# A two-layer transformer trunk step: 62 modulation units go from VectorE to TensorE, and their weight loads are placed anew

## The chip, the cores and the metric

One core of one Trainium2 chip runs the whole program. The metric is the device time of one execution in microseconds (us). The engines are named as in the profile: PE is TensorE (matmuls; PEld its weight loads), DVE is VectorE, ACT is ScalarE, POOL is GpSimd, and SP is SyncE, whose queue issues nearly all transfers.

## The reference, cut to what matters

The trunk has two layers. Each layer is a feed-forward half, a token mixer, and a second feed-forward half. 640 tokens (512 latent, 128 context) have 1024 features. Ahead of every sub-layer its input is modulated, and its output is gated:

```python
def _modulation(cond, w, b):
    return (jax.nn.silu(cond) @ w + b).reshape(cond.shape[0], N_MOD, D_MODEL)

def _modulate(x, shift, scale):
    return x * (1.0 + scale[:, None, :]) + shift[:, None, :]

def _residual_post_norm(x, f, gate, weight, g, b):
    return _layernorm(DN_ALPHA * x + weight * gate[:, None, :] * f, g, b)

def _ffn_half(x, mod, slot, w1, w3, w2, g, b):
    h = _modulate(x, mod[:, 3 * slot], mod[:, 3 * slot + 1])
    f = (jax.nn.silu(h @ w1) * (h @ w3)) @ w2
    return _residual_post_norm(x, f, mod[:, 3 * slot + 2], FFN_RES, g, b)
...
for l in range(DEPTH):
    mod_p = _modulation(c_ctx[None, :], w_mod[l], b_mod[l])   # context tokens
    mod_s = _modulation(c, w_mod[l], b_mod[l])                # latent tokens
```

There are 9 modulation vectors of 1024 values in each layer, for two condition vectors (`c` and `c_ctx`): a product of a 1024 x 9216 weight matrix with two vectors, once for each layer. This product is what the change is about. The hidden width of a feed-forward half is 2816. The mixer has three groups of heads: A (differential attention, 4 heads), B (windowed attention, 8 heads) and C (latent attention, 4 heads).

## The kernel before, in words

**A modulation unit** is one vector of a layer in one tile of 128 features, `(l, s, d)`, for both conditions. There are 2 x 9 x 8 = 144 units, and each reads 512 KB of weights. A unit can be computed on two engines.

On TensorE, `mod_mm` (L391) issues 8 matmuls (16 instructions): the silu of the conditions, `silc`, stands in 32 columns, the 128 features stream past it, and four 32-column groups write four quarters of the partitions of a PSUM bank. The result is copied to SBUF as `ms`, and a matmul with `sel` adds the four quarters and puts the features on partitions. In a mixer this is done in the unused part of a bank that holds one transposed block of probabilities: `t5` (L1578, L1707) issues that transpose and then calls `mod_beside` (L411). `mod_beside` issues the `sel` matmul of the unit before (L415) and the matmuls of the next unit (L397), and leaves two steps on ScalarE for later, the addition of the bias (L422) and the copy to `ms` (L425). Each unit's weights come in two transfers of 256 KB to the pool `wm` of four buffers, so to the room of two units; `mod_load(k)` (L365) issues what is missing of the next `k` units.

On VectorE, the generator `vec_mods` (L437) multiplies the transposed weights, `wv`, with the conditions, `cb`, and sums: four instructions over 512 columns (L460) and a small one (L463) for a unit. The transfers `wv` use the same four buffers.

**A feed-forward half** (`ffn`, L1016) runs through its 22 hidden tiles in six chunks. Most hidden tiles are a `Pair` (L830): seven products instead of eight (Winograd's scheme), each of 12 matmuls of 320 columns (L847), whose results VectorE adds and subtracts into `pm`, `sl` and `gf` (L858) as their banks fill. A chunk ends with the products with `w2` (L485), which VectorE adds to `x` (L610). The weights are split into a high and a low part on the fly, the high part on ScalarE (L299), the low part on VectorE or GpSimd (L306). After the first chunk's first pair, `mods` (L1025) is called 95 times in a half; each call moves `vec_mods` on by `(4 * nvec + 4) / 95` steps. In the first chunk of layer 0's first half, 8 units run on TensorE as well. At the end of a half, `norm` (`rows_norm`, L659) makes the layer norm and, tile by tile, opens the next phase's first products (L656).

**A mixer** (`mixer`, L1192) works on 48 attention units (a tile of 128 queries, for a head of group A or C or for two heads of group B), which pass through scores, exponentials, transposes and values. The order of all their steps is written out by hand in `SCHEDULES`, one string for each layer: `r7` is the step `t5` of unit 7, with `mod_beside` in it, `q7` copies that bank's transposed block to SBUF, and `R7` does what `mod_beside` left for ScalarE. `mod_beside` is called in all 16 units of A and all 16 of C, and in the 8 units of B whose keys take three blocks. That is 40 places in each mixer. `mix_left` (L1925) says how many of them get a unit: before the change 10 in layer 0 and none in layer 1. In group C, four transfers for every pair of heads take the outputs of some queries to the other half of the partitions (`hl_c`, L1802; `move`, L1256); they stand on SP's queue among the loads.

Each engine executes its instructions in the order in which they were issued, and so does SP with its transfers, each waiting there for its buffer.

The numbers of units are set where the trunk is put together:

```python
h, first = ffn(l, 0, h, first, *((8, 38) if l == 0 else (0, 36)), ...)
if l == 0:
    modq += [vecq.pop(0) for _ in range(10)]
h, first = mixer(l, h, first, ...)
...
h, first = ffn(l, 1, h, first, 0, 36 if l == 0 else 0, ...)
```

Of the kernel before, what the change touches and what calls it, by code (L numbers as in the profile page):

```python
# [15 lines left out]
P = 128  # L16
D = 1024
KD = D // P
T = 640
# [86 lines left out]
def trunk_kernel(tc, I, O):  # L106
# [3 lines left out]
    with ExitStack() as es:  # L110
# [98 lines left out]
        class W:  # L209
            """a weight tile in pieces along its contraction tiles"""  # L210
# [9 lines left out]
        class Stream:  # L220
            """jobs in the order of their products: whole tiles, or the blocks a pair of tiles is combined to"""
# [28 lines left out]
            def combine(self, r):  # L250
                """the sums of Winograd's scheme of two tiles' halves along the contraction"""
# [74 lines left out]
        tasks = []  # L326
# [10 lines left out]
        def step(n=1, fill=1):  # L337
            """the oldest task's next steps, as many of the filler, and a waiting transfer"""
            for _ in range(n):
                advance(tasks)  # L340
            for _ in range(fill):
                advance(filler)
            if dmaq:
                dmaq.pop(0)()

        def start(g):
            """a task whose first step comes at once"""
            next(g)
            tasks.append(g)
# [8 lines left out]
        modq = []  # L358
        mod_queue = [nc.sync]
        mod_depth = [2]  # L360
# [30 lines left out]
        def mod_mm(ps):  # L391
# [6 lines left out]
            mod_load(mod_depth[0])  # L398
# [7 lines left out]
        def mod_start():  # L406
            """128 modulation values of the next unit, before they are put on partitions"""
            ps = bank("mod")
            mod_take(mod_mm(ps[:, :P]), ps[:, :P])

        def mod_beside(ps):  # L411
            """the same in the unused part of a bank; gives what is left to do when the bank's products are issued"""
# [16 lines left out]
        def mod_step():  # L429
            """the rest of the last unit, and the start of the next"""  # L430
# [6 lines left out]
        def vec_mods(n):  # L437
            """generator: the next n units on the vector engine, beside the products of a feed-forward half"""
# [41 lines left out]
        def mmk(out, whl, acts, half, k, ka, n):  # L480
            """the three passes of contraction tile k (of n) into a half's bank"""
# [19 lines left out]
        def acc(d, half):  # L501
            """running sums of x and x^2 over feature tiles"""
# [27 lines left out]
        def bcast(name, src, nt):  # L530
            """[P, nt] per-token values (token on its partition) to every partition, along the tokens"""
# [34 lines left out]
        def mod_hi(d, half, h):  # L566
            """hi part of x * gamma + beta"""
# [5 lines left out]
        def mod_f(d, half, kept=None):  # L573
            """x * gamma + beta, in kept when it is to stay"""
# [56 lines left out]
        def rows(acts, n, begun, each):  # L631
            """x += gate * (w^T act) for every feature tile; begun: (weights, sums, contraction tiles done) of the first ones"""
# [17 lines left out]
        def open_tiles(pn, wn, h, half, d):  # L650
            """contraction tile d of the next phase's first weight tiles, the passes that need hi first"""
# [7 lines left out]
        def rows_norm(acts, n, l, ln, nxt, begun=()):  # L659
            """the same, then the layer norm; with nxt = (layer, slot), also the next modulated input and, tile by tile  # L660
            as it comes, the first weight tiles of the next phase; begun: (weights, sums, contraction tiles done) of the
            first feature tiles"""
# [62 lines left out]
            # first half: statistics under the second half's products  # L725
# [76 lines left out]
        def alpha_x(l, ln):  # L802
            """the residual branch of what the norm left in x"""
# [9 lines left out]
        later = []  # L813

        def slot():
            """what waited for the products issued so far"""
# [13 lines left out]
        class Pair:  # L830
            """silu(w1^T h) * (w3^T h) of one hidden tile by Winograd's scheme: rows w1, w3, columns the halves of the tokens"""
# [94 lines left out]
            def run_first(self, mods, other, ts):  # L926
                """the same with the sums of the input's quarters last, as they come, and the start of the other one before them"""
# [43 lines left out]
        def tb_steps(tb, h):  # L971
            """generator: hi and lo of the sums of the input's quarters, for the contraction tiles k and k + 4; the last ones
            take the place of the quarter that no pair reads"""
# [152 lines left out]
        def tr_issue(items, odd=None):  # L1126
            """PE transposes of [q, 128-key] blocks, four to a bank (a fifth alone goes to the bank odd)"""
# [25 lines left out]
        def pvm(blocks, po, vs):  # L1153
            """po [q, 64 per head] = sum over keys, head after head"""
# [4 lines left out]
        def scaled(dst, po, r):  # L1159
            """dst [q, two heads of 64] = po * r per query and head"""  # L1160
# [3 lines left out]
        def to_hl(on, g=None):  # L1164
            """hi and lo of the transpose of on [token tiles, 128 features]"""
# [26 lines left out]
        def mixer(l, h, first, norm):  # L1192
# [6 lines left out]
            # x waits in memory while the attention needs its room  # L1199
# [37 lines left out]
            def rope(dst, q0, cos, sin, m):  # L1237
                """dst (512 columns) = q0 * cos + partner * sin; q0 is overwritten"""
# [12 lines left out]
            def rope_k(kk, q0, cos, sin, m):  # L1251
                """keys in the order s0 s1 ctx s2 s3"""
# [948 lines left out]
```

## Time and profile before

| what | us |
|---|---|
| three timed runs, lowest, median, highest | 2775.0, 2775.86, 2776.04 |
| span of the profiled execution, from its first to its last instruction | 2768.7 |
| TensorE busy in it (weight loads) | 2541.8 (2430.0) |
| VectorE busy | 2257.6 |
| ScalarE busy | 1150.4 |
| GpSimd busy | 1249.4 |

The page gives the profiled execution by its span alone; its own time from start to end is not listed. The busy time of an engine is the sum over all stages. Where an engine waits, the profile names what ended the wait.

### The profile page before, as it was taken

The numbers are of one execution on the slowest core, as the hardware profiler recorded it, in microseconds if no ns is written. First come the engines' busy times: TensorE is split into PE (matmuls) and PEld (weight loads), VectorE is DVE, ScalarE is ACT, GpSimd is POOL, SyncE is SP. The second block draws the span as 40 slices with busy tenths as digits, with TensorE's granted clock in tenths as the row PEclk, the third lists the DMA queues.
The fourth block names the chain that finished last, engine by engine and source line by source line (L and its number), as shares of the span: only waits on it lengthen the run. The fifth ranks groups of instructions, "written<-read, shape, count | busy, mean of one in ns | idle before, by whom it ended". The sixth has DMA issues, their size and how long they took to land. (4 is left out here: it accounts for less than half of the span.)

```text
span 2768.7 us, 48136 instructions
## 1 busy us (share of the span) xinstructions
PE 2541.8 (92%) x17546; PEld 2430.0 (88%) x17546; DVE 2257.6 (82%) x4315; ACT 1150.4 (42%) x2474; POOL 1249.4 (45%) x973
## 2 busy tenths in 40 slices
PE   7998899899999998888999988998898899999997
PEld 6988899888868998888889888898897689999997
DVE  6699999865875889999988999999677758777776
ACT  5232323345575533333344333333455745344333
POOL 2343453521454644434545445434333556545545
PEclk9999999999999999999989999999999999999998
DMA  7333333334212133333323333333332121222222
GB/s 265 129 120 109 115 113 125 114 118 149 74 37 92 69 115 118 122 103 112 118 69 103 116 119 113 119 126 99 120 100 60 37 99 47 82 78 89 81 85 69
DMA packets 130539, 285.77 MB, mean 103 GB/s; under 512 B 16832, under 2 KB 34560, under 8 KB 129664
## 3 DMA queue, kind: packets, MB, share of 16 engines
q1 hardware_dynamic: 130304, 282.70, 31.3%
q8 instruction: 139, 2.28, 0.3%
q14 instruction: 96, 0.79, 0.1%
HBM read 254.95 MB, written 8.81 MB: 95 GB/s over the span
## 5 line engine op out<-in xcount | busy, mean ns | idle before, releaser
L306 DVE TENSOR_TENSOR wl<-wr,wh 128x512 fp32r<-128x512 f32 (+1 forms) x524 | 499.0, 965 | 66.3 <-ACT wh L299 64.5
L299 ACT CAST wh<-wr 128x512 fp32r<-128x512 f32 (+1 forms) x570 | 331.9, 606 | 500.8 <-DMA wr<-in_w 351.8
L485 PE MATMUL o<-gh,wh 128*128 128x256 f32 (+1 forms) x1408 | 442.8, 314 | 24.8 <-ACT gh L886 13.2
L847 PE MATMUL p<-hh,wh 128*128 128x320 f32 x1216 | 387.7, 319 | 83.3 <-DVE pm L858 79.1
L485 PE MATMUL o<-gl,wh 128*128 128x256 f32 (+1 forms) x1408 | 440.7, 313 | 3.2 <-DVE gl L478 1.8
L259 POOL TENSOR_TENSOR ws<-wr 128x512 f32<-128x512 f32 x76 | 111.3, 1464 | 728.4 <-DMA wr<-in_w 548.8
L485 PE MATMUL o<-gh,wl 128*128 128x256 f32 (+1 forms) x1408 | 438.1, 311 | 0.0
L460 DVE SCALAR_TENSOR_TENSOR scr<-wv,cb 128x512 f32<-128x512 f32 x440 | 394.7, 897 | 4.2
L847 PE MATMUL p<-hl,wh 128*128 128x320 f32 x1216 | 384.7, 316 | 6.6 <-DVE hl L1010 6.6
L847 PE MATMUL p<-hh,wl 128*128 128x320 f32 x1216 | 385.5, 317 | 1.9 <-DVE wl L306 1.8
L847 PEld LDWEIGHTS p<-hh,wh 128*128 128x128 f32 x1216 | 235.6, 194 | 92.3 <-issue 78.0
L306 POOL TENSOR_TENSOR wl<-ws,wh 128x512 fp32r<-128x512 f32 x152 | 241.4, 1595 | 133.3 <-ACT wh L299 133.3
L485 PEld LDWEIGHTS o<-gh,wh 128*128 128x128 f32 x1408 | 269.3, 191 | 33.6 <-ACT gh L886 16.0
L299 ACT CAST wh<-ws 128x512 fp32r<-128x512 f32 x304 | 181.3, 619 | 247.3 <-POOL ws L259 80.6
L485 PEld LDWEIGHTS o<-gl,wh 128*128 128x128 f32 x1408 | 269.5, 191 | 8.9 <-DVE gl L891 4.9
L485 PEld LDWEIGHTS o<-gh,wl 128*128 128x128 f32 x1408 | 269.1, 191 | 0.0
L610 DVE SCALAR_TENSOR_TENSOR x<-o,gat,x 128x128 f32<-128x128 f32 (+2 forms) x404 | 192.8, 523 | 92.9 <-PE o L485 87.4
L847 PEld LDWEIGHTS p<-hl,wh 128*128 128x128 f32 x1216 | 236.1, 194 | 7.6 <-DVE hl L1010 7.6
L847 PEld LDWEIGHTS p<-hh,wl 128*128 128x128 f32 x1216 | 235.9, 194 | 4.0 <-DVE wl L306 4.0
L877 ACT ACTIVATE sl<-sl 128x320 f32<-128x320 f32 x76 | 35.8, 471 | 277.7 <-DVE sl L858 277.5
L259 POOL TENSOR_TENSOR ws<-wr,ws 128x512 f32<-128x512 f32 x76 | 130.8, 1720 | 0.0
L306 DVE TENSOR_TENSOR wl<-ws,wh 128x512 fp32r<-128x512 f32 x152 | 129.3, 863 | 0.0
(428 smaller groups left out, 6618.8 us busy)
## 6 DMA issues: line engine op xcount, KB each, us to landing
wr<-in_w SPq DMA_DIRECT2D x176, 512.0 KB, 3.8
wv<-in_wmt SPq DMA_DIRECT2D x220, 256.0 KB, 2.8
wr<-in_w SPq DMA_DIRECT2D x128, 256.0 KB, 2.6
wm<-in_wmod SPq DMA_DIRECT2D x68, 256.0 KB, 5.0
wr<-in_w SPq DMA_DIRECT2D x64, 192.0 KB, 2.4
wr<-in_wint SPq DMA_DIRECT2D x24, 512.0 KB, 3.8
wr<-in_wo SPq DMA_DIRECT2D x16, 512.0 KB, 3.8
xd<-x SPq DMA_DIRECT2D x16, 320.0 KB, 5.6
```

Source lines behind the costliest of these rows:

```text
L259: G.tensor_tensor(out=o, in0=x0, in1=x1, op=op)
L299: S.copy(hl[0], src[:, c0:c1])
L306: eng.tensor_tensor(out=t2, in0=src, in1=t.bitcast(F32), op=ALU.subtract)
L460: V.scalar_tensor_tensor(out=scr, in0=w[2 * i + hf], scalar=1.0, in1=cb[:, 2 * st + hf, :], op0=ALU.mult, op1=ALU.mult, accum_out=a[:, 2 * ...
L485: PE.matmul(out[:, :cn], whl[a][:, k, :], b[:, c0:c0 + cn], start=k == 0 and i == 0, stop=k == n - 1 and i == 2)
L610: V.scalar_tensor_tensor(out=c, in0=src, scalar=gat[:, d, s:s + 1], in1=c, op0=ALU.mult, op1=ALU.add)
L847: PE.matmul(out[:, :HN], w[a][:, k, :], b[k][c], start=k == 0 and i == 0, stop=k == 3 and i == 2)
L877: S.activation(self.sl[:, HI], self.sl[:, HI], AF.Silu)
```

## The change

Of the 120 units that come after the first 24, VectorE gets 16 in each of the first three feed-forward halves (before: 38, 36 and 36), the mixer of layer 0 gets 40 (before: 10) and the mixer of layer 1 gets 32 (before: none). The units stay in the order in which they are needed. The second edit is in `mod_mm`: the load behind a unit's matmuls now asks for one unit ahead and not for two, so that the transfers of the unit after the next are issued ahead of the next unit's matmuls. While the first products run, the depth is 6 on both sides as before. The other lines of the diff only blank comments.

```diff
-        mod_depth = [2]
+        mod_depth = [2, 2]
...
         def mod_mm(ps):
             mod_load(mod_depth[0])
             unit = modq.pop(0)
             w = modw.pop(unit)
             for kk in range(2):
                 for g in range(4):
                     PE.matmul(ps[32 * g:32 * g + 32, :], silc[:, 2 * g + kk, :], w[g // 2][:, 2 * (g % 2) + kk, :], start=kk == 0, stop=kk == 1)
-            mod_load(mod_depth[0])
+            mod_load(mod_depth[1])
             return unit
...
-            mod_depth[0] = 6
+            mod_depth[:] = 6, 6
...
-                mod_depth[0] = 2
+                mod_depth[:] = 2, 1
...
-            h, first = ffn(l, 0, h, first, *((8, 38) if l == 0 else (0, 36)), lambda a, n, b: rows_norm(a, n, l, 0, (l, 1), b),
+            h, first = ffn(l, 0, h, first, 0 if l else KD, 2 * KD, lambda a, n, b: rows_norm(a, n, l, 0, (l, 1), b),
                            alpha_first if l == 0 else lambda: alpha_x(l - 1, 2), tb, ts)
-            if l == 0:
-                modq += [vecq.pop(0) for _ in range(10)]
+            modq += [vecq.pop(0) for _ in range((4 if l else 5) * KD)]
             h, first = mixer(l, h, first, lambda a, n, b: rows_norm(a, n, l, 1, (l, 2), b))
...
-            h, first = ffn(l, 1, h, first, 0, 36 if l == 0 else 0, lambda a, n, b: rows_norm(a, n, l, 2, nxt, b),
+            h, first = ffn(l, 1, h, first, 0, 0 if l else 2 * KD, lambda a, n, b: rows_norm(a, n, l, 2, nxt, b),
                            lambda: alpha_x(l, 1), tb, ts)
```

The first place is VectorE in the middle of layer 0's second feed-forward half, from one pair's last additions to the next pair's. `scr` is the output of a unit's step, `wl` a low part of weights. First before the change:

```order
L858 TENSOR_TENSOR pm_13208<-pm_13208,p_13251 128x320
L306 TENSOR_TENSOR wl_13350<-ws_13318,wh_13349 128x512
L858 TENSOR_TENSOR sl_13269<-pm_13208,p_13347 128x320
L306 TENSOR_TENSOR wl_13374<-ws_13316,wh_13373 128x512
L460 SCALAR_TENSOR_TENSOR scr_11428,va_13292<-wv_13184,cb_10852 128x512 x2
L881 TENSOR_TENSOR gf_13344<-gf_13344,sl_13269 128x320
L858 TENSOR_TENSOR sl_13429<-pm_13367,p_13371 128x320
L306 TENSOR_TENSOR wl_13414<-wr_13324,wh_13413 128x512
L463 SCALAR_TENSOR_TENSOR mod_145<-va_13292,const 128x2
L460 SCALAR_TENSOR_TENSOR scr_11428,va_13451<-wv_13248,cb_10852 128x512
L306 TENSOR_TENSOR wl_13434<-wr_13324,wh_13433 128x512
```

And the same place on VectorE after the change:

```order
L858 TENSOR_TENSOR pm_13374<-pm_13374,p_13414 128x320
L306 TENSOR_TENSOR wl_13512<-ws_13480,wh_13511 128x512
L858 TENSOR_TENSOR sl_13432<-pm_13374,p_13509 128x320
L306 TENSOR_TENSOR wl_13536<-ws_13478,wh_13535 128x512
L460 SCALAR_TENSOR_TENSOR scr_11797,va_13454<-wv_13197,cb_11114 128x512
L881 TENSOR_TENSOR gf_13506<-gf_13506,sl_13432 128x320
L858 TENSOR_TENSOR sl_13590<-pm_13529,p_13533 128x320
L306 TENSOR_TENSOR wl_13575<-wr_13486,wh_13574 128x512
L306 TENSOR_TENSOR wl_13595<-wr_13486,wh_13594 128x512
```

Of three steps of units and a small addition, one step is left here; the rest of the order is the same.

The second place is TensorE in the mixer of layer 0, at a unit of group C: `tr` and `t` are the banks of the transposes, `sc` the next unit's scores. First before the change:

```order
L1133 MATMUL tr_9637<-idn,ec_9608 128x128 x4
L1580 MATMUL t_9644<-idn,ec_9608 128x128
L1629 MATMUL sc_9648<-C0kh_9284,C0qh_9282 128x320
L1629 MATMUL sc_9648<-C0kl_9285,C0qh_9282 128x320
L1629 MATMUL sc_9648<-C0kh_9284,C0ql_9283 128x320
```

And a unit of the same group on TensorE after the change:

```order
L1133 MATMUL tr_9766<-idn,ec_9724 128x128 x4
L1580 MATMUL t_9776<-idn,ec_9724 128x128
L415 MATMUL t_9776<-const,ms_9715 128x2
L397 MATMUL t_9776<-wm_9751,silc 32x128 x2
L397 MATMUL t_9776<-wm_9753,silc 32x128 x2
L397 MATMUL t_9776<-wm_9751,silc 32x128 x2
L397 MATMUL t_9776<-wm_9753,silc 32x128 x2
L1629 MATMUL sc_9793<-C0kh_9272,C0qh_9270 128x320
L1629 MATMUL sc_9793<-C0kl_9273,C0qh_9270 128x320
L1629 MATMUL sc_9793<-C0kh_9272,C0ql_9271 128x320
```

Behind the fifth transposed block there now stand the `sel` matmul of the unit before and the matmuls of the next unit.

The third place is SP's queue in the same mixer and group: the last transfers of keys and queries (`C1`), then the moves of outputs (`oh`). First before the change:

```order
L1890 DMA C1qh_9417<-qph_8614 32x512
L1891 DMA C1kh_9419<-kph_8479 32x640
L1890 DMA C1ql_9418<-qpl_8615 32x512
L1891 DMA C1kl_9420<-kpl_8480 32x640
L1256 DMA oh_9527<-oc_9529 64x2x128 x2
L1256 DMA oh_9527<-oc_9676 64x2x128 x2
```

And the same place on SP's queue after the change, up to the first move and the loads behind it:

```order
L1890 DMA C1qh_9466<-qph_8532 32x512
L1891 DMA C1kh_9468<-kph_8371 32x640
L1890 DMA C1ql_9467<-qpl_8533 32x512
L1891 DMA C1kl_9469<-kpl_8372 32x640
L374 DMA wm_9532<-in_wmod 128x512
L374 DMA wm_9534<-in_wmod 128x512
L374 DMA wm_9590<-in_wmod 128x512
L374 DMA wm_9592<-in_wmod 128x512
L1256 DMA oh_9608<-oc_9610 64x2x128 x2
L374 DMA wm_9644<-in_wmod 128x512
L374 DMA wm_9646<-in_wmod 128x512
```

The unit weights now stand between the transfers of this group, two transfers for a unit, and some of them behind a move that waits for ScalarE's copy `oc`.

## Rows read from the trace of the kernel before

**Rows 1.** The page: span, then busy us of each engine (share) xinstructions.

```profile
span 2768.7 us, 48136 instructions
PE 2541.8 (92%) x17546; PEld 2430.0 (88%) x17546; DVE 2257.6 (82%) x4315; ACT 1150.4 (42%) x2474; POOL 1249.4 (45%) x973
```

**Rows 2.** Source lines L1110 and L527, from 948: duration min/median/max ns, first and last start.

```profile
L1110 DVE TENSOR_SCALAR gat<-mod x1: 162/162/162, 992.8 to 992.8; 128x16 f32<-128x16 f32 x1
...
L527 PE MATMUL st<-onesd,ys x10: 242/352/370, 1423.6 to 1437.5; 128*128 128x1 f32 x10
```

**Rows 3.** Windows of the halves: length; PE, PEld, DVE, ACT, POOL busy; clock, DMA, GB/s.

```profile
110.70:542.70 432.00, 390.63 (x2507) 379.06 (x2506) 403.38 (x768) 138.72 (x262) 190.11 (x118) 0.97 0.36 120
992.80:1423.60 430.80, 389.25 (x2513) 380.05 (x2512) 401.05 (x751) 138.64 (x262) 191.10 (x118) 0.96 0.35 115
1508.60:1935.50 426.90, 386.34 (x2498) 376.67 (x2496) 399.46 (x751) 138.29 (x262) 191.19 (x118) 0.97 0.36 119
2373.90:2742.30 368.40, 366.67 (x2507) 366.36 (x2506) 268.32 (x422) 138.92 (x253) 179.44 (x118) 1.00 0.24 79
```

**Rows 4.** TensorE's waits, 948 to 1423.6: us in total, times, longest.

```profile
PE p L847 <- DVE pm L858: 27.3, 10, 4.4
```

**Rows 5.** TensorE's waits, 2329.3 to 2742.3, the longest.

```profile
PE p L847 <- DVE hl L1010: 2.0, 1, 2.0
```

**Rows 6.** Windows of 6 us in the second half; columns as in group 3.

```profile
1042.00:1048.00 6.00, 1.75 (x12) 1.49 (x11) 5.96 (x8) 1.69 (x3) 4.95 (x3) 1.00 0.11 33
1048.00:1054.00 6.00, 5.83 (x29) 5.86 (x30) 5.86 (x16) 1.41 (x4) 0.00 (x0) 0.72 0.24 79
```

**Rows 7.** Windows: the mixers of layer 0 and layer 1.

```profile
583.00:911.40 328.40, 305.48 (x2462) 274.23 (x2462) 214.99 (x474) 183.19 (x500) 129.21 (x138) 0.98 0.32 96
...
1974.50:2292.80 318.30, 296.39 (x2277) 266.74 (x2276) 215.84 (x474) 178.30 (x480) 131.19 (x138) 0.98 0.27 81
```

**Rows 8.** Windows 2410:2422, 2470:2482, 2530:2554, 2602:2626, 2686:2710: their sum and mean.

```profile
sum 96.00, PE 96.00 PEld 96.00 DVE 90.81 ACT 47.57 POOL 72.43; mean PE 19.20 PEld 19.20 DVE 18.16 ACT 9.51 POOL 14.49
```

**Rows 9.** Timeline of TensorE in layer 0's mixer: start, us, instruction xcount.

```profile
644.00 0.60 PE L1133 MATMUL tr<-idn,e 128*128 128x128 f32 x4
644.36 0.54 PE L1600 MATMUL sa<-rp,rp 128*128 128x320 f32 x2
...
644.85 0.28 PE L415 MATMUL t<-const,ms 128*128 128x2 f32 x2
645.06 0.64 PE L397 MATMUL t<-wm,silc 128*32 128x128 f32 x16
645.63 0.56 PE L1600 MATMUL sa<-rp,rp 128*128 128x320 f32 x2
```

**Rows 10.** Source lines L425 and L422: duration min/median/max ns, first and last start.

```profile
L425 ACT COPY ms<-t x10: 258/263/278, 637.8 to 701.5; 128x128 f32<-128x128 f32 x10
L422 ACT ACTIVATE mod<-t,const x10: 262/266/268, 641.1 to 708.3; 128x2 f32<-128x2 f32 x10
```

**Rows 11.** ScalarE's waits, 630 to 705: us in total, times, longest.

```profile
ACT mod L422 <- PE t L397: 8.2, 5, 4.7
ACT pt L1142 <- PE t L397: 8.2, 4, 3.6
```

**Rows 12.** TensorE's waits, 630 to 705.

```profile
PE t L397 <- DMA wm<-in_wmod: 2.8, 2, 2.6
PE pj L485 <- ACT pt L1142: 0.6, 2, 0.4
```

**Rows 13.** Source line L1580 in layer 0's mixer, the units of group C.

```profile
L1580 PE MATMUL t<-idn,ec x16: 270/272/330, 818.2 to 863.3; 128*128 128x128 f32 x16
```

**Rows 14.** Tile `wm` on SP, 600 to 720: issue ns, then landing in us.

```profile
L374 SPq DMA_DIRECT2D wm<-in_wmod x20: 328/377/853, 624.5 to 687.6; - x20
...
DMA to landing us min/median/max: 2.6/2.9/6.7
```

**Rows 15.** SP's waits, whole span: us in total, times, longest.

```profile
SPq L1256 <- ACT oc L1799: 66.4, 13, 10.2
```

## The prediction, made before the change was timed

> **What bounds the kernel now.** The page's first two lines give the span, 2768.7 us, and the busy shares: TensorE 92% (its weight loads 88%), VectorE 82% [rows 1]. That average hides stages with different limits, so I read stage by stage next. The three timed runs have a median of 2775.86; the page gives the profiled execution its span alone, so I take the 7.2 us between the two as what lies around the span and add it at the end.
>
> The four feed-forward halves contain the same products, and only the last has no units on VectorE. I cut each half from the gate's copy at the end of its first chunk (the copy L1110; VectorE units start about there) to the first statistics matmul of its norm (L527); [rows 2] shows both marks for the second half, 992.8 and 1423.6. [rows 3] puts the four stretches side by side: 432.0, 430.8, 426.9 and 368.4 us for about 2507 matmuls each. The reader is to see that in the last one TensorE is busy 366.67 of 368.40 us at a clock of 1.00 with VectorE at 268.3 us, and that in the other three VectorE is busy 399 to 403 us, 93% of the stretch, while TensorE idles some 41 us. So VectorE bounds the first three and TensorE the last.
>
> The waits say how. In the second half TensorE waits 27.3 us for VectorE's additions on `pm`, ten times, up to 4.4 us [rows 4]; in the last half the longest wait in the list is 2.0 us [rows 5]. A wait costs more than itself: from 1042 to 1048 TensorE is busy 1.75 of 6 us, and in the next 6 us its granted clock is 0.72 [rows 6], a mixture of its two levels, 1.2 and 2.4 GHz.
>
> The mixers are near TensorE's limit too. From the end of the opened products to the first statistics, layer 0's takes 328.4 us with 10 units and layer 1's 318.3 with none, TensorE busy 93% in both [rows 7].
>
> **What is taken away.** 62 units leave VectorE: 22 in the first half, 20 each in the second and third. The stretches give a unit's price there: (401.05 - 268.32)/36 = 3.69 us [rows 3]. Sixteen cost 59.0, so VectorE's work becomes 268.3 + 59.0 = 327.3. At the 93.1% that VectorE reached before, that would need 351.6 us, less than the 368.4 that TensorE needs: TensorE becomes the bound, and the saving can't exceed 63.6 + 62.4 + 58.5 = 184.5 us.
>
> Not all of that comes, since VectorE's other work is bunched. Sixteen units take 59.0/368.4 = 16% of VectorE throughout (a step comes at a fixed rate of calls), which leaves 10.08 of every 12 us. I cut the last half into 31 windows of 12 us; in eight of them VectorE's own work is above that. Joined, these eight are the windows of [rows 8]: 90.8 us of work against 96 x 0.84 = 80.6. The 10.2 us over I count in full as lost in each half, although the PSUM banks give VectorE some slack, because of what a wait does to the clock. Each stretch then takes 378.6 us and the saving is 53.4 + 52.2 + 48.3 = **153.9 us**. Bounds: no loss, 184.5; or TensorE's loss shrinks only as the number of units, 63.6 x 22/38 + (62.4 + 58.5) x 20/36 = 104.0. I lie nearer the first, because after the change VectorE is no longer full on average.
>
> **What is added.** The same 62 units go to TensorE in the mixers (30 more in layer 0, 32 in layer 1): 16 matmuls and the pair with `sel`. Where nothing waits these take 0.57 us (645.06 to 645.63) and 0.21 us (644.85 to 645.06), 0.78 together [rows 9]: 48.4 us for 62. The difference of the two mixers gives more, 10.1 us for 10 units [rows 7], waits and the two layers' different orders included. I take that, **62.6 us**, because it includes what a unit does to its neighbours.
>
> The 16 matmuls start 36 ns apart, where the four full-width transposes above them start 90 ns apart (644.00 to 644.36) [rows 9]. The Trainium skill's TensorEngine Tiling (Array Packing), Overview, says that stationary operands of at most 32 columns can share the array four ways, for up to four times the speed; this unit's operands are 32 wide, and the trace agrees in direction with a factor of 2.5. Unpacked, at 90 ns each, 62 units would cost 102 us instead of 48.4.
>
> ScalarE gets 62 copies of 0.26 and 62 additions of 0.27 us [rows 10], 33 us in all; it is busy only 183 of 328 us in the mixer [rows 7], so the work itself hides. Its order is the danger: with 10 units ScalarE waited 16.4 us for TensorE's unit matmuls [rows 11], 1.64 per unit, with later exponentials queued behind. If all of that reached the end, a unit would cost 0.78 + 1.64 and the mixers 150 us; TensorE's own waits behind it were only 0.6 us [rows 12], so I leave it out of the sum.
>
> The loads stay 512 KB a unit and as many, but 124 of them move on SP's queue from the halves into the mixers, and a unit's load now stands just ahead of the preceding unit's matmuls instead of behind those of the one before. It still needs the same buffers. In the units of 3 us at the end of the mixer (latent group C, 16 from 818.2 to 863.3 [rows 13]) two issues and a landing of 2.9 us median [rows 14] take 3.7 us for a place that is reused every two units: hidden. But in four places (three in layer 0, one in layer 1) a move of `oh` now stands ahead of a load, and SP waited up to 10.2 us for ScalarE at such moves [rows 15]. I price each of the four, and the first unit of layer 1, like the worst wait for a unit's weights, 2.6 us [rows 12]: **13.0 us**. Below: nothing, if SP is early enough. Above: all 62 units wait like that, a rival.
>
> The first half's eight units by the direct route, the first chunk's products, and the tails of the norms change by nothing that I can price: the same instructions, under the same products.
>
> **Sum.** 2768.7 - 153.9 + 62.6 + 13.0 = 2690.4, and 7.2 around it: **2698 us**, 2.8% faster.
>
> **Rivals.** *VectorE's waits shrink only in proportion* (104.0 saved): its interruptions, not its fill, delay TensorE. For it: each step, 0.9 us (a quarter of 3.69), stands in line ahead of urgent additions; against it: VectorE was nearly always full around the waits. 2775.9 - 104.0 + 75.6 = 2747.
>
> *Everything fits*: 184.5 saved, 48.4 paid: 2640.
>
> *The mixers starve for unit weights* (the other side): every one of 62 units waits 2.6 us on TensorE, in order, so that all behind it waits. For it: the one load that came late cost that; 512 KB per 3 us is 175 GB/s beside what the mixer moves already. Against it: eight of the first ten units hardly waited [rows 12]. 2775.9 - 153.9 + 62 x (0.78 + 2.6) = 2832. It decides from 153.9/62 - 0.78 = 1.7 us a unit.
>
> *TensorE is the bound everywhere*: what leaves VectorE gives nothing and TensorE's new work is paid in full, 2775.9 + 48.4 = 2824. Against it: the 62 us between equal halves [rows 3]. The Trainium skill's Perfetto Trace Analysis, Identifying the Most-Contended Engine, takes the engine of highest occupancy, TensorE judged by its weight loads, and by 88% against 82% would call this a move in the wrong direction; the stretches do not agree.
>
> *The two sides cancel*: 104 saved and about as much paid in the mixers, through ScalarE's order: 2776.
>
> **How the numbers follow.** Forecast 0.68; proportional 0.12; all fits 0.08; starved 0.05; TensorE everywhere 0.03; cancel 0.04. A difference of 0.2% is about what a measurement of this kernel can tell from none. The forecast and the first two rivals are faster, 0.88; cancel is the same, 0.04; the other two slower, 0.08. The forecast's own range, from its bounds (no loss and 48.4 on one side, half the way to the proportional saving and 20 us of waits on the other), is 2655 to 2735. With the proportional rival and the good end inside, the range is 2640 to 2758, with 0.12 outside.
>
> **What would show it.** The three stretches at 370 to 390 us with VectorE near 327 and TensorE's waits on `pm` under 10 us each; the mixers near 364 and 355 us; unit matmuls waiting for their weights at few places, those behind the `oh` moves. Wrong if the stretches stay above 400 us, or if the mixers' waits list puts the unit weights at the head with 50 us or more.

## The result, and the profile after

The changed kernel takes 2693.93 us (median of four runs, 2690.66 to 2705.26) beside 2775.95 for the kernel before: ratio 0.9707, with an interval of 0.9678 to 0.9736. The forecast was 2698. That the sum hit is partly luck: it was 24 us too low in the halves, and 15 us too high in the mixers and 5 us around the span.

The page of the changed kernel, span and busy times, beside [rows 1]:

```profile
span 2703.3 us, 49877 instructions
PE 2555.0 (95%) x18662; PEld 2453.0 (91%) x18662; DVE 2072.3 (77%) x3759; ACT 1175.9 (43%) x2596; POOL 1244.0 (46%) x973
```

TensorE does 1116 matmuls more (62 units of 18) and is busy 13 us longer; VectorE is busy 185 us less. The windows of the changed kernel, cut at the same marks as [rows 3] and [rows 7]: three halves with units, the last half, the two mixers:

```profile
111.60:499.60 388.00, 374.79 (x2509) 371.29 (x2507) 339.94 (x571) 140.45 (x262) 190.72 (x118) 0.99 0.32 103
976.00:1366.40 390.40, 376.54 (x2513) 372.42 (x2512) 340.11 (x572) 141.07 (x262) 190.09 (x118) 0.99 0.32 100
1452.40:1837.20 384.80, 373.03 (x2504) 369.74 (x2504) 339.92 (x572) 141.13 (x262) 188.63 (x118) 0.99 0.33 105
2308.90:2677.30 368.40, 366.71 (x2507) 366.39 (x2506) 267.50 (x422) 138.58 (x253) 178.22 (x118) 1.00 0.25 79
537.10:893.80 356.70, 331.88 (x2998) 296.96 (x2997) 216.24 (x476) 192.25 (x558) 129.97 (x138) 0.98 0.44 132
1877.80:2227.50 349.70, 326.45 (x2854) 291.31 (x2853) 213.60 (x474) 188.85 (x544) 130.26 (x138) 0.97 0.41 122
```

The halves came down from 427 to 432 us to 385 to 390, the granted clock in them rose from 0.96 and 0.97 to 0.99, the last half did not move, and each mixer grew by some 30 us. What the reader should see in the first three rows: VectorE is far from full (340 of 388) and TensorE still idles 12 to 14 us, as it does not in the fourth row.

This profiled execution was the slowest of the four. Where a size matters below I use a second profile of the same kernel (the first experiment), whose span is 2697.2 us and whose time is 2699.16. Its three halves with units and its two mixers:

```profile
113.40:498.10 384.70, 372.80 (x2507) 369.68 (x2505) 338.37 (x570) 140.71 (x261) 189.24 (x118) 0.99 0.33 103
977.90:1365.10 387.20, 375.41 (x2510) 371.68 (x2508) 339.38 (x571) 140.07 (x261) 188.33 (x118) 0.99 0.32 101
1448.10:1835.70 387.60, 375.92 (x2512) 371.97 (x2510) 338.04 (x571) 140.34 (x261) 190.95 (x118) 0.99 0.32 104
535.60:895.80 360.20, 334.74 (x2998) 299.55 (x2997) 216.36 (x476) 192.37 (x558) 129.84 (x138) 0.97 0.44 131
1873.10:2219.90 346.80, 324.60 (x2855) 289.87 (x2853) 212.84 (x474) 189.04 (x544) 130.73 (x138) 0.98 0.41 123
```

The same mixer differs by up to 3.5 us between the two profiles. One mark needs a correction: in [rows 7] the window of layer 0's mixer starts at 583.0, 0.9 us before the last of the opened products (583.9). Cut there, as in all other runs, the mixer of the kernel before is 327.6 us, and not 328.4.

TensorE's waits in the changed kernel's second half, beside [rows 4] (us in total, times, longest):

```profile
PE p L847 <- DVE pm L858: 5.7, 3, 2.0
PE o L485 <- ACT gh L886: 4.8, 5, 1.1
```

The 27.3 us of ten waits for `pm` are 5.7 of three. What is left stands in a few places. The windows around two of these waits (columns as in [rows 3]), and the two waits themselves:

```profile
1144.00:1156.00 12.00, 12.00 (x84) 12.00 (x83) 11.90 (x16) 3.69 (x7) 7.93 (x6) 1.00 0.36 109
1156.00:1168.00 12.00, 10.06 (x69) 9.82 (x69) 11.90 (x19) 4.93 (x10) 6.47 (x4) 1.00 0.24 68
1312.00:1324.00 12.00, 10.44 (x72) 10.17 (x70) 12.00 (x16) 5.66 (x11) 9.27 (x7) 1.00 0.08 28
1324.00:1336.00 12.00, 11.60 (x69) 11.63 (x70) 10.81 (x23) 3.67 (x8) 0.99 (x1) 0.86 0.31 87
```

```profile
1161.89 0.39 PE L847 MATMUL p<-hh,wh 128*128 128x320 f32 x1 [1.94 <-DVE pm L858]
1324.40 0.38 PE L847 MATMUL p<-hh,wh 128*128 128x320 f32 x1 [1.96 <-DVE pm L858]
```

Of the five busy columns the third is VectorE: it is full (11.90, twice, and 12.00) with GpSimd busy beside it; TensorE then idles 1.6 to 1.9 us, and in the last row its clock is 0.86, a mixture of its two levels. That is the bunching of the prediction, with a larger price than its 10.2 us in a half.

### The profile page after: what moved, and what is told of

It reads as the page before. It is cut to its first block, busy times and chain, and to the rows that moved or that the text cites. A ratio compares the mean times of both kernels' runs of the same rounds, so it can differ in the third digit from the quotient of the medians.

```text
span 2703.3 us, 49877 instructions
## 1 busy us (share of the span) xinstructions
PE 2555.0 (95%) x18662; PEld 2453.0 (91%) x18662; DVE 2072.3 (77%) x3759; ACT 1175.9 (43%) x2596; POOL 1244.0 (46%) x973
## 5 line engine op out<-in xcount | busy, mean ns | idle before, releaser
L306 DVE TENSOR_TENSOR wl<-wr,wh 128x512 fp32r<-128x512 f32 (+1 forms) x524 | 518.3, 1003 | 74.1 <-ACT wh L299 72.5
L485 PE MATMUL o<-gh,wh 128*128 128x256 f32 (+1 forms) x1408 | 439.5, 312 | 19.4 <-ACT gh L886 11.7
L847 PE MATMUL p<-hh,wh 128*128 128x320 f32 x1216 | 378.4, 311 | 16.8 <-DVE pm L858 16.8
L847 PE MATMUL p<-hl,wh 128*128 128x320 f32 x1216 | 378.2, 311 | 6.2 <-DVE hl L1010 6.2
L847 PE MATMUL p<-hh,wl 128*128 128x320 f32 x1216 | 378.1, 311 | 0.0
L847 PEld LDWEIGHTS p<-hh,wh 128*128 128x128 f32 x1216 | 229.9, 189 | 19.0 <-issue 18.9
L847 PEld LDWEIGHTS p<-hl,wh 128*128 128x128 f32 x1216 | 230.0, 189 | 7.4 <-DVE hl L1010 7.4
L847 PEld LDWEIGHTS p<-hh,wl 128*128 128x128 f32 x1216 | 230.0, 189 | 0.3 <-DVE wl L306 0.3
L460 DVE SCALAR_TENSOR_TENSOR scr<-wv,cb 128x512 f32<-128x512 f32 x192 | 181.2, 944 | 0.0
L259 POOL TENSOR_TENSOR ws<-wr,wr 128x512 f32<-128x512 f32 x76 | 130.2, 1713 | 0.0
L259 POOL TENSOR_TENSOR ws<-ws,wr 128x512 f32<-128x512 f32 x76 | 119.1, 1567 | 6.0
```

The costliest lines, as they stand in the source:

```text
L259: G.tensor_tensor(out=o, in0=x0, in1=x1, op=op)
L306: eng.tensor_tensor(out=t2, in0=src, in1=t.bitcast(F32), op=ALU.subtract)
L460: V.scalar_tensor_tensor(out=scr, in0=w[2 * i + hf], scalar=1.0, in1=cb[:, 2 * st + hf, :], op0=ALU.mult, op1=ALU.mult, accum_out=a[:, 2 * ...
L485: PE.matmul(out[:, :cn], whl[a][:, k, :], b[:, c0:c0 + cn], start=k == 0 and i == 0, stop=k == n - 1 and i == 2)
L847: PE.matmul(out[:, :HN], w[a][:, k, :], b[k][c], start=k == 0 and i == 0, stop=k == 3 and i == 2)
```

## The experiments

Times in one group of runs are compared with the kernel before, timed beside them (2779.25, 2777.59 and 2778.59 us in the three groups). "Stretches" are the first three halves, cut as above.

**The changed kernel once more** (first group). 2695.53 us, ratio 0.9707 [0.9681, 0.9733]; stretches 384.7, 387.2 and 387.6, last half 369.1, mixers 360.2 and 346.8. 

> The changed kernel itself, timed once more beside the others. Both theories: 2694 within 6 us, since its four runs lay between 2690.7 and 2705.3. It is the yardstick for the other runs of this chip, and gives a second profile, because the first one (span 2703.3) was that of the slowest run.

 It is the yardstick for what follows.

**No units in the mixers.**

```diff
+        for m_ in mod:
+            V.memset(m_, 0.0)
...
-            modq += [vecq.pop(0) for _ in range((4 if l else 5) * KD)]
+            del vecq[:(4 if l else 5) * KD]
```

> Leaves the 72 units of the mixers uncomputed (their modulations stay zero); the halves are as in the changed kernel. Theory 1, a unit in a mixer costs what the two mixers showed, 0.97 us with its waits: 72 x 0.97 = 70 us less than the changed kernel, 2624; both mixers near 318 us. Theory 2, the mixers hide a part of the units in TensorE's waits and only the bare 0.78 us or less counts: 56 us less or fewer, 2638 or more. Theory 3, the units also disturb what follows them (ScalarE's order, the transfers): more than 80 us less, below 2614.

2634.2 us, ratio 0.9479 [0.9457, 0.9502]: 61 us less than the changed kernel. The two mixers:

```profile
537.60:861.10 323.50, 296.60 (x2277) 267.27 (x2277) 215.80 (x474) 179.96 (x480) 129.48 (x138) 0.98 0.28 80
1837.60:2156.90 319.30, 296.56 (x2277) 266.93 (x2276) 216.25 (x474) 178.49 (x480) 131.37 (x138) 0.98 0.29 81
```

They shrink by 707.0 - 642.8 = 64.2 us, 0.89 for each of 72 units. This price includes the transfers of their weights, which are gone too. Without units layer 0's mixer takes 323.5, not 318.3: the two layers differ by 4 us by themselves. Of the 10.1 us that I gave to the ten units of the kernel before [rows 7], only 327.6 - 323.5 = 4.1 are theirs.

**No units on VectorE.**

```diff
-            h, first = ffn(l, 0, h, first, 0 if l else KD, 2 * KD, lambda a, n, b: rows_norm(a, n, l, 0, (l, 1), b),
+            del vecq[:2 * KD]
+            h, first = ffn(l, 0, h, first, 0 if l else KD, 0, lambda a, n, b: rows_norm(a, n, l, 0, (l, 1), b),
```

The other call of `ffn` likewise. 

> Leaves the 48 units of VectorE uncomputed; the mixers are as in the changed kernel. Theory 1, the rest of VectorE's work crowds TensorE only where it is bunched: the three stretches fall from 388, 390 and 385 us to the 368 of the last half, 57 to 60 us less, 2635. Theory 2, the rest of the loss has another cause (weights coming late, the mixers' transfers reaching into the halves, the clock): the stretches stay above 380 us and the time falls by less than 25 us, above 2669.

2653.88 us, ratio 0.9542 [0.9521, 0.9563]. Its three stretches:

```profile
112.10:482.80 370.70, 368.19 (x2508) 367.99 (x2507) 270.49 (x427) 140.96 (x258) 179.00 (x118) 1.00 0.27 85
962.20:1333.20 371.00, 368.09 (x2514) 367.42 (x2512) 272.52 (x427) 140.83 (x257) 178.80 (x118) 1.00 0.27 83
1415.00:1785.80 370.80, 368.23 (x2508) 368.03 (x2508) 269.91 (x428) 140.87 (x258) 177.96 (x118) 1.00 0.27 86
```

The stretches met the first theory, 2 us from the last half. The time fell by 42 us rather than the 57 to 60 expected. Against the second profile the stretches give 1159.5 - 1112.5 = 47: they end at 371 and not at 368 (7 us), and the expectation had counted from the slower first profile (4 us). The mixers of this run's profile are 360.5 and 350.3, 4 us longer together than in the second profile, which makes up most of the rest. So the 16 units of a half cost it 16 us.

**28 units in each half, 20 and 16 in the mixers.**

```diff
-            modq += [vecq.pop(0) for _ in range((4 if l else 5) * KD)]
+            modq += [vecq.pop(0) for _ in range(16 if l else 20)]
```

and `28` for `2 * KD` in both calls of `ffn`. 

> The same 120 units, divided 28, 28, 28 on VectorE and 20 and 16 in the mixers. Theory 1, a threshold (VectorE delays TensorE little until it is full): VectorE's work of 268 + 28 x 3.69 = 372 us needs about 399 at the 93% it reached, so the stretches take 400 to 406, 45 us more in the three; the mixers get 36 units fewer, 35 us less: 2704. Theory 2, in proportion (each unit on VectorE costs TensorE 1.7 us from the first on): stretches of 417, 87 us more, 35 less: 2746.

2744.55 us, ratio 0.9874 [0.9852, 0.9897]; stretches 406.5, 406.5 and 410.4, mixers 344.6 and 338.5. The stretches are nearly the first theory's, the total is the second's: 36 units fewer in the mixers gave back 23.9 us, not 35. With 0, 16 and 28 units a stretch takes 370.8, 386.5 and 407.8 us on average, and 429.9 with the 36 to 38 of the kernel before [rows 3]: 1.0, 1.8 and some 2.5 us for each unit more. The saving is neither a constant per unit nor a bound reached at once.

**A rate that follows VectorE's load.** The units' steps come faster in the calls between the `w2` products and slower in those beside the pairs:

```diff
-                    credit[0] += (4 * nvec + 4) / 95 * (1 if when is None else 1)
+                    credit[0] += (4 * nvec + 4) / 95 * (1.6 if when is None else 0.55)
```

> The same units on the same engines as in the changed kernel, but a step on VectorE is worth 1.6 of the even rate in a call between products with w2, where VectorE's own work is light, and 0.55 in a call between a pair's products, where it is heavy. Theory 1, the rest of the loss in the halves comes from bunched VectorE work: the stretches fall from 385 to 390 us to about 378, 25 to 35 us less, 2664. Theory 2, the loss goes with the number of steps and not with their place: 2694 within 4 us.

2665.25 us, ratio 0.9612 [0.9589, 0.9635]:

```profile
112.20:488.90 376.70, 371.23 (x2507) 369.65 (x2506) 326.26 (x571) 139.86 (x262) 189.57 (x118) 0.99 0.33 105
967.30:1342.80 375.50, 368.65 (x2503) 366.02 (x2501) 329.34 (x571) 139.93 (x261) 190.49 (x118) 1.00 0.33 104
1425.80:1802.70 376.90, 370.55 (x2512) 367.69 (x2511) 328.54 (x571) 140.11 (x261) 190.03 (x118) 1.00 0.34 107
```

The same units in the same halves cost 5.6 us a half in place of 15.7, and VectorE is busy some 11 us less for them (328 in place of 339). In the second half TensorE's waits for `pm`, 5.7 us in the changed kernel, are gone:

```profile
PE p L847 <- DVE pm L858: 0.2, 1, 0.2
```

That the loss goes with the place of the units and not with their number is shown. Why the place matters is not: steps in a calm stretch find spare time on VectorE, but they also take less time there (last section).

**Loads right behind the unit's matmuls.** The part of the change that moves the loads is undone:

```diff
-                mod_depth[:] = 2, 1
+                mod_depth[:] = 2, 2
```

> The changed kernel with the load placement of before: two units are asked for behind a unit's matmuls. Theory 1, placement matters little, because a load needs the same buffers either way and the moves behind it are not what TensorE waits for: 2694 to 2702. Theory 2, the placement carries the change: SP then stands before a unit's matmuls at every unit and the attention's moves come late: 2715 or more.

2683.87 us, ratio 0.9675 [0.9647, 0.9703]. Both theories missed: this part of the change is a loss. The intervals of this run and of the changed kernel overlap, but the mixers are shorter beyond the 3.5 us of scatter, and the same edit is worth 15 us in the version with both edits below, with intervals that do not overlap. The mixers:

```profile
538.10:889.50 351.40, 329.49 (x2998) 295.88 (x2997) 216.15 (x476) 192.33 (x558) 129.32 (x138) 0.98 0.45 134
1869.40:2213.20 343.80, 323.50 (x2855) 289.98 (x2854) 215.40 (x474) 189.24 (x544) 130.64 (x138) 0.98 0.42 124
```

They take 695.2 in place of 707.0, 11.8 us less. The medians differ by as much, 11.7, though across two groups of runs: by the ratios it is 9. How a load comes late in the changed kernel shows in its second profile, on SP's queue and then on TensorE:

```profile
656.32 5.76 SPq L1256 DMA_DIRECT2D kb<-kb  x6
662.17 1.03 SPq L374 DMA_DIRECT2D wm<-in_wmod  x2
663.26 3.47 SPq L1256 DMA_DIRECT2D kz<-bkp  x4
666.83 0.53 SPq L243 DMA_DIRECT2D wr<-in_wqup  x1
```

```profile
666.54 0.41 PE L397 MATMUL t<-wm,silc 128*32 128x128 f32 x4 [3.07 <-DMA wm<-in_wmod]
```

The pair of issues at 662.17 is behind six moves of `kb` that took 5.8 us to issue, and TensorE waits 3.07 us for what they load. With each load issued right behind the matmuls that free its buffer, the queue holds the same moves, but TensorE finds its weights there. In layer 0's mixer TensorE waited 8.1 us, eight times, for `wm` in the changed kernel; here it waits 3.0 us, twice, both at the first unit. In both mixers together the waits for `wm` fall from 13.6 to 4.5 us, 9 of the 11.8.

**Half of the weights.** A load of 256 KB serves both halves of a unit, with four units' loads ahead:

```diff
-                    for hf in range(2):
+                    for hf in range(1 if mod_pool[0] is pm else 2):
...
-                    modw[unit] = w
+                    modw[unit] = w * (2 // len(w))
...
-                mod_depth[:] = 2, 1
+                mod_depth[:] = 4, 3
```

> Each unit on TensorE loads only the first 256 KB of its weights and uses them twice (so the modulations are those of half the weights), and the four buffers hold four units. Theory 1, the waits for unit weights in the mixers cost what the waits list shows, 15 us in the mixers of both layers, and a little for the clock: 12 to 20 us less, 2677. Theory 2, TensorE's matmuls alone make the price of a unit: 2694 within 4 us.

2674.74 us, ratio 0.9646 [0.9619, 0.9673]; mixers 351.0 and 340.5. It is the first theory's number, but read with the experiment above: the earlier loads alone shorten the mixers by 11.8 us, and this edit, which halves the bytes and loads further ahead at once, by 3.7 more, about as much as two profiles of one kernel differ.

**ScalarE's part of a unit on VectorE.**

```diff
-                    S.activation(mod[l][:, s, d, :], ps[:, P:P + 2], AF.Identity, bias=bmod[:, l, s, d:d + 1])
+                    V.tensor_scalar(mod[l][:, s, d, :], ps[:, P:P + 2], bmod[:, l, s, d:d + 1], None, ALU.add)
...
-                    S.copy(ms, ps[:, :P])
+                    V.tensor_copy(ms, ps[:, :P])
```

> The two steps that a unit leaves to ScalarE (copy and bias) go to VectorE. Theory 1, ScalarE's waits for the units (63 us in the two mixers) lie beside TensorE's work: 2694 within 5 us. Theory 2, they delay exponentials and copies that TensorE needs next, and a unit's price above the bare 0.78 us comes from them: 10 to 30 us less, below 2684.

2696.99 us, ratio 0.9729 [0.9704, 0.9754], mixers 358.5 and 353.7: no gain. In the changed kernel's first mixer ScalarE waits 30 us for units (beside 16.4 in [rows 11]):

```profile
ACT pt L1142 <- PE t L397: 17.9, 8, 4.5
ACT mod L422 <- PE t L397: 12.1, 8, 5.5
```

But in the run without ScalarE's two steps such waits are still there. In its first mixer ScalarE's copies of the transposed blocks (`pt`) wait 36 us, for VectorE's copy `ms` and for the units' matmuls:

```profile
ACT pt L1142 <- DVE ms L425: 20.6, 7, 4.5
ACT pt L1142 <- PE t L397: 15.6, 8, 3.2
```

So the run shows that the unit's two instructions on ScalarE cost nothing that can be measured. It did not take the waits away, so it does not show what they cost.

**Both edits together** (rate 1.6 and 0.55, `mod_depth` 2, 2). 

> Both of the earlier edits together: VectorE's units are stepped 1.6 times as fast in the calls between the w2 products and 0.55 times in the calls beside the pairs, and a unit's loads stand again right behind the unit's matmuls. Theory 1 (the bunching in the halves and the late weight loads in the mixers are two separate losses in two separate stretches): they add, 2665 less 10 to 12, so 2653 to 2655; stretches 375 to 377, mixers 343 to 352. Theory 2 (both edits recover the same wait on SP's queue or on the buffers that the units of both kinds share, so the second gives little): 2660 to 2666.

2649.92 us (2647.19 to 2655.33), ratio 0.9555 [0.9537, 0.9574]: 4.4% faster than the kernel before, and the best of all here that do the whole work. Stretches 375.9, 375.3 and 374.8, mixers 347.5 and 344.0. The two losses lie in separate stretches and add, as the first theory said; the time is 3 us better than its range.

**The load placement alone, in the kernel before** (`mod_depth` 2, 1 there, nothing else). 

> The kernel before with the change's load placement and nothing else: in the mixers a unit's loads stand ahead of the preceding unit's matmuls. Layer 0's mixer has 10 units, layer 1's none. Theory 1 (a late load costs about what the 5th experiment gave back, 10 to 12 us over 72 units, so 0.15 a unit): 0 to 3 us slower than before, layer 0's mixer 328 to 331. Theory 2 (the placement costs per queue jam, not per unit): up to 6 us slower. Theory 3 (the placement helps where units are few): 1 to 3 us faster.

2776.54 us, ratio 0.9999 [0.9986, 1.0012]; mixers 330.3 and 318.9. With ten units the placement costs nothing that can be told from zero, as the first theory allows; the 2.7 us in layer 0's mixer (327.6 before, from the right mark) are in the direction of a loss, but within the scatter between two profiles. A jam of 6 us is excluded, and so is a gain of over 4.

**A steeper rate**, 2.2 and 0.1, with `mod_depth` 2, 2. 

> As the first of this call, with a steeper rate: 2.2 between the w2 products and 0.1 beside the pairs. Theory 1 (the loss left in each half, some 5 to 6 us over the half without units, still comes from units beside the pairs): stretches 371 to 374, time 2643 to 2650. Theory 2 (it is now made between the w2 products, where VectorE gets full in its turn, or the 1.6 and 0.55 already level the load): stretches 377 to 385, time 2655 to 2680.

2654.99 us, ratio 0.9564 [0.9546, 0.9582]; stretches 377.1, 375.2 and 376.2. No better than 1.6 and 0.55, and not the 371 to 374 of the first theory: with next to no steps beside the pairs a half still loses 5 us over one without units. Whether that is what was left before, or a new loss between the `w2` products as the second theory has it, is not shown.

**24 units in each half**, 28 and 20 in the mixers, with both edits. 

> As the first of this call, with 24 units in each of the three halves and 28 and 20 in the mixers (after: 16 and 40, 32). Theory 1 (with the rate levelled, a unit costs a half what 16 cost it by the 4th experiment, (376.4 - 370.8)/16 = 0.35 us, and its price stays near that until VectorE is full on average, 267.5 + 24 x 3.7 = 356 of 368): stretches 378 to 382, mixers 20 us less by 0.85 a unit, time 2640 to 2650. Theory 2 (the price is convex well before VectorE is full, as with 28 uneven ones): stretches 386 to 395, time 2665 to 2690.

2690.53 us, ratio 0.9694 [0.9676, 0.9712], 41 us slower than with 16:

```profile
111.60:503.30 391.70, 374.85 (x2507) 368.20 (x2506) 359.40 (x642) 139.65 (x262) 191.85 (x118) 1.00 0.36 113
963.80:1361.50 397.70, 380.51 (x2510) 373.01 (x2509) 361.65 (x643) 139.98 (x262) 191.38 (x118) 0.98 0.35 109
1445.30:1839.70 394.40, 376.98 (x2510) 370.39 (x2508) 363.29 (x643) 139.93 (x262) 191.18 (x118) 0.99 0.36 113
```

The first theory falls: eight units more cost a stretch 19 us, 2.4 each, though VectorE's 361 us would fit into 368. With the levelled rate the price is 0.3 us a unit up to 16 and 2.4 from there to 24; somewhere between VectorE at 327 and at 361 us of work the cover ends.

## Why the prediction was right, and where it was not

The forecast's sum beside the second profile of the changed kernel, in us:

| part | predicted | measured |
|---|---|---|
| three halves with units | 3 x 378.6 = 1135.8 | 1159.5 |
| two mixers | 646.7 + 62.6 + 13.0 = 722.3 | 707.0 |
| last half | 368.4 | 369.1 |
| the rest of the span | 463.9 | 461.6 |
| around the span | 7.2 | 2.0 |
| sum | 2697.6 | 2699.2 |

**VectorE bounds the three halves, TensorE the last.** Right: without units on VectorE the stretches fall to 371 us, and 62 units fewer gave 130.2 of the 184.5 us that lay above the last half. As the sign that was named, TensorE waited for `pm` under 6 us in each of the three.

**"The 10.2 us over I count in full as lost in each half."** The mechanism was right, the size was not: a half lost 18 us over the last half, 16 over a half without units. Two things were too small. VectorE's sixteen units were taken at the mean price of 36, 59.0 us, and its work at 327.3; it was 338 to 340. And the loss was taken as VectorE's surplus alone, whereas TensorE idled 10 us more than in the last half and its busy time was 7 us longer, at a granted clock of 0.99 (second profile). The levelled rate brought VectorE to 326 to 329 us, what the forecast had, and the loss to 8 us over the last half. The 130.2 us lie midway between the forecast's 153.9 and the 104.0 of the proportional rival, so the changed kernel alone would not have told the two apart; the experiments with other numbers and places of units do.

**"I take that, 62.6 us, because it includes what a unit does to its neighbours."** This step failed, by the choice between two numbers. Of the 10.1 us between the mixers, 4.1 were the ten units'; the rest was the layers' own difference (323.5 and 319.3 without units), the early mark, and scatter. Of the 64.2 us that 72 units cost, 11.8 are late loads; the other 52.4 are 0.73 a unit, beside the bare 0.78 from the timeline [rows 9]. By the bare price, 48.4 + 13.0 = 61.4, the mixers would have been forecast within 1.1 us of the measured growth of 60.3.

**Late loads, 13.0 us.** The size was right, 11.8 measured, but by luck, since the places were not: of the four moves of `oh` that were named, one made TensorE wait 0.96 us and another at most 0.28; the largest wait, 3.07, came behind moves of `kb`, and others elsewhere. The first unit of layer 0, not of layer 1 alone, waited 2.6. A load can come late behind other moves of SP's queue too, not those of `oh` alone.

**ScalarE's order, left out of the sum.** Right, though not by the experiment that was made for it, in which ScalarE still waits. It is read from the price: with both edits the mixers take 691.5 us, 48.7 more than without units, so 0.68 a unit. That is below the bare 0.78, which leaves nothing to be seen of the 1.64 a unit that ScalarE's order might have added.

**7.2 us around the span.** Wrong: it is 2.0 (2699.16 - 2697.2). The other 5 us are most likely the difference of the profiled execution from the median, since the kernel before has ranged from 2766 to 2786 us.

**The forecast's own range.** Its bounds, 2655 and 2735, do not come out of the parts named for them: no loss and 48.4 give 2640, or 2653 with the late loads, and half the way to the proportional saving with 20 us of waits gives 2730. The range of 2640 to 2758 does not rest on them.

**The rivals.** Waits that shrink only in proportion (2747) missed the time by 53 us and are excluded by the 160.6 us that the levelled rate saves with the same units, but their idea, that VectorE's interruptions count as well as its fill, holds in part: the convex price and the rate's effect show it. Starvation (2832): the weight waits of TensorE in both mixers come to some 14 us for 72 units, not 2.6 each. TensorE as the bound everywhere (2824) falls too, since the halves are some 40 us shorter each. The Trainium skill's Perfetto Trace Analysis, Identifying the Most-Contended Engine, takes the engine of highest occupancy for the one to relieve; over the whole span that would be TensorE, but here the weight loads' share went up from 88% to 91% and the kernel became 3% faster. Cancelling (2776) fell as well, by the time.

**What stays open.** Why a half with 16 levelled units still takes 5 us more than one without. Whether the levelled rate gains by VectorE's spare time or by the shorter instructions below was not separated; the steeper rate, with VectorE at 331 us and no less time, does not settle it. The 2.5 us that TensorE still waits at the first unit of layer 0's mixer, in the version with both edits, could go with a load ahead of the mixer; that was not tried.

## What to carry to other kernels

The price of filler work on a nearly full engine was convex here: take its units away until the price of the next one is that of its new place (here 0.7 to 0.9 us), and step the rest where that engine has room, not at a fixed rate. Put a transfer right behind the last use of its buffer, since everything that is issued in between stands ahead of it on its queue. To price a unit from two stages, first ask what the stages differ by without it.

## What the runs showed of the hardware that was not expected

The same VectorE instruction can take 2.6 times as long when GpSimd works beside it. VectorE and GpSimd in the changed kernel's second half, by start and length:

```profile
1148.40 1.70 DVE L460 SCALAR_TENSOR_TENSOR scr<-wv,cb 128x512 f32<-128x512 f32 x1
...
1152.83 1.78 DVE L460 SCALAR_TENSOR_TENSOR scr<-wv,cb 128x512 f32<-128x512 f32 x1
...
1156.04 0.47 DVE L858 TENSOR_TENSOR sl<-pm,p 128x320 f32<-128x320 f32 x1
...
1163.93 0.68 DVE L460 SCALAR_TENSOR_TENSOR scr<-wv,cb 128x512 f32<-128x512 f32 x1
```

```profile
1148.25 1.30 POOL L306 TENSOR_TENSOR wl<-ws,wh 128x512 fp32r<-128x512 f32 x1 [1.31 <-ACT wh L299]
1152.22 1.84 POOL L259 TENSOR_TENSOR ws<-wr 128x512 f32<-128x512 f32 x1 [2.67 <-DMA wr<-in_w]
...
1155.73 1.55 POOL L259 TENSOR_TENSOR ws<-wr,wr 128x512 f32<-128x512 f32 x1
...
1158.94 3.54 POOL L306 TENSOR_TENSOR wl<-ws,wh 128x512 fp32r<-128x512 f32 x2
```

A unit's multiplication is 1.70 and 1.78 us beside GpSimd's instructions, 0.68 at 1163.93 with GpSimd idle since 1162.48; the addition that reads `p` in PSUM is 0.47 beside GpSimd too. Both long ones end 0.55 us after GpSimd's instruction does (1150.10 and 1149.55; 1154.61 and 1154.06): they look blocked, not slowed. The whole half bears it out: of its 64 multiplications 17 take over 0.9 us, and each of these starts while a GpSimd instruction runs and ends 0.54 to 0.56 us after that one. Working beside GpSimd is not enough by itself, since 13 of the 47 short ones also start while GpSimd runs. The Trainium skill's SBUF — State Buffer, in "SBUF: two separate sides", says that a VectorE instruction with two inputs in SBUF and a GpSimd instruction that reads SBUF exclude each other, whichever starts first, for its whole length; the rows of the long ones agree.

It reaches small instructions too: the units' last step, on 128 x 2 numbers, takes from 0.21 to 1.34 us in the second half of the changed kernel. This step and the multiplications, there and then in the version with both edits:

```profile
L460 DVE SCALAR_TENSOR_TENSOR scr<-wv,cb 128x512 f32<-128x512 f32 x64 | 61.4, 959 | 0.0
...
L463 DVE SCALAR_TENSOR_TENSOR mod<-va,const 128x2 f32<-128x2 f32 x16 | 10.1, 630 | 0.0
```

```profile
L460 DVE SCALAR_TENSOR_TENSOR scr<-wv,cb 128x512 f32<-128x512 f32 x64 | 56.0, 874 | 0.1
...
L463 DVE SCALAR_TENSOR_TENSOR mod<-va,const 128x2 f32<-128x2 f32 x16 | 4.7, 292 | 0.1
```

10.8 us of the 13 by which VectorE's busy time differs between these two halves (340.1 and 327.2) are these two lines. That GpSimd is the cause is read from the rows; no run took GpSimd's work away. A VectorE instruction's price from one stage need not hold in another where GpSimd does something else beside it.
